# Splitting the bit-by-bit top-k search of a sparse-attention layer into three groups instead of two

## The chip, the cores and the metric

The kernel runs on one core of one Trainium2 chip. The metric is the device time of one execution in microseconds (us). The kernel before was timed in 3 runs: 1661.65, 1662.74 and 1662.96 us, a median of 1662.74 us. A separate execution was recorded by the hardware profiler. A core has five engines that each work through a queue of their own in order: PE (matrix products), DVE (vector work), ACT (activation functions, casts and copies), POOL (more vector work) and SP (which issues transfers).

## The reference, cut to what matters

The layer has two attention branches, a gate for each and a feed-forward part. Branch A attends sparsely: an indexer scores every key for every query, and only the best `topk` keys take part. There are 1024 prompt positions (topk 256) and 32 sample positions that also see a cache of 512 keys (topk 136).

```python
def dsa_block(q, q_i, w_i, qpos, k, v, k_i, topk):
    s_idx = jnp.einsum('bqhd,bld->bqhl', q_i, k_i).astype(jnp.float32)
    score = jnp.einsum('bqhl,bqh->bql', jax.nn.relu(s_idx), w_i.astype(jnp.float32))
    admissible = (kpos // CHUNK)[None, :] <= (qpos // CHUNK)[:, None]
    score = jnp.where(admissible[None], score, -jnp.inf)
    _, idx = lax.top_k(score, topk)
    ...
    p = jax.nn.softmax(logits, axis=-1)
    return jnp.einsum('bqhk,bqkhd->bqhd', p.astype(v.dtype), vg)
```

Everything else (the projections, the second branch, the gates, the feed-forward part) is dense matrix work around this.

## The kernel before, in words

The 1056 positions are cut into 9 tiles: tiles 0 to 7 hold 128 prompt positions each, and tile 8 holds the 32 sample positions. Query tile t of the prompt sees 128(t+1) keys, and tile 8 sees 544. Tiles 0 and 1 have at most 256 keys and need no search. For tiles 2 to 8 the kernel makes the scores (`index_scores`, line 955): PE writes products into three PSUM banks called `s`, ACT applies relu in place, and DVE adds the weighted result into a `score` tile. Tiles 2, 3, 4 and 8 come first there, and 5, 6 and 7 later.

Then it finds for each query the k-th largest score by setting the 31 bits of a float from the top down (`top_k_begin`, line 984). For each bit DVE makes a candidate threshold (`cand`, an xor on the threshold `thr`), the scores below it are counted for each tile, DVE compares the counts with what is wanted (`hit`), and `thr` takes the candidate where the comparison holds (`copy_predicated`). `thr`, `hit` and the wanted counts lie in a PSUM tile called `small`. A count is a pass over a tile's scores: on DVE a compare with an accumulated sum, followed by a read of the accumulator; on ACT a sign function with an accumulated sum. Tiles 5, 6 and 7, the longest, are counted on ACT, and 2, 3, 4 and 8 on DVE.

The tiles are put in groups, and one candidate, one comparison and one conditional copy serve all tiles of a group, side by side in its columns. The table `TOPK` (line 53) names each group, its tiles, those of them that ACT counts, and its place in `small`. Before there are two groups: "a" with tiles 2, 3, 4 (DVE) and 7 (ACT), and "b" with 5 and 6 (ACT) and 8 (DVE). So each group's comparison waits for counts of both engines. After the search `top_k` (line 1053) turns each threshold into a mask, tile by tile, in the order of the groups: a few passes on ACT and, on DVE, a scan and a comparison into the tile `pre`, with one more pair of passes into `pen` for tiles that ACT counted.

The order of all instructions is made when the program is built. Every operation is recorded with a rank (FAST for emptying PSUM, PREP for loads, MAIN, FILL for matrix products that fill PE's time, SLOW for the search), and a list scheduler (`Plan.run`, line 371) lets each engine take the ready operation of the best rank, by a table of costs. On the chip each engine then runs its list strictly in that order. While the search runs, PE makes the dense projections: of branch B and the first gates (`project_b`, `gate`) and then of branch A (`project_a`). Their results lie in two PSUM banks `pj` (and the three `s`), and DVE empties them in rows whose outputs are called `zb`, `vt`, `gz` and `ta`; these are called evictions below and are counted from the start of the program. Branch B's attention starts after the masks are done, its k, q, v and weight tiles use the memory that the search frees.

Of the kernel before, what the change touches and what calls it, by code (L numbers as in the profile page):

```python
# [49 lines left out]
FWORDS = 3200  # L50
PACE = 16
PA_BANKS = ('s', 'pj', 's', 's', 'pj')
TOPK = (("a", [2, 3, 4, 7], (7,), 0), ("b", [5, 6, 8], (5, 6), 16))
QUARTER = T // 4
QUADS = ((QUARTER, 0), (QUARTER, 2 * QUARTER))
B11, B21, T1, T2, T3, T4, B22 = range(7)
# [404 lines left out]
class Layer:  # L461
# [522 lines left out]
    def top_k_begin(self):  # L984
# [59 lines left out]

        self.groups = [Group(*x) for x in TOPK]
        self.size = size
# [1004 lines left out]
```

## Time and profile before

| | us |
|---|---|
| median of 3 runs | 1662.74 |
| the profiled execution, its own time | 1660.59 |
| the span of its instructions | 1658.8 |
| PE busy in the span | 1648.2 (99%) |
| DVE busy in the span | 1296.7 (78%) |
| ACT busy in the span | 988.7 (60%) |
| first search count on DVE that reads a candidate (start) | 176.0 |
| last search count on DVE (start) | 336.0 |

The span runs from the first to the last instruction of the program; the execution's own time has 1.79 us around it. A row of a timeline gives a start and a duration in us, the engine, the operation, what it writes and reads by the program's names (`junk<-score,cand` is a count, `small<-cnta,small` the comparison of group a, `small<-small,cand` the conditional copy), the shapes, and in brackets how long the engine sat idle before it and what released it. Nearly all rows stand under line 441, since one helper issues every operation. Rows of matrix products overlap each other, so the pace of PE is read from one start to the next.

### The profile page before, as it was taken

How to read it: one execution, taken by the hardware profiler on the slowest of the kernel's cores; microseconds unless marked ns; L12 is line 12 of the kernel's file. 1: busy time of each engine (PE TensorE's matmuls, PEld its weight loads, DVE VectorE, ACT ScalarE, POOL GpSimd, SP SyncE). 2: the span in 40 equal slices, each digit the busy share in tenths (PEclk: the TensorE clock that was granted, in tenths of full speed). 3: DMA queues.
4: the chain of work that ended last, by engine and by line, in shares of the span. 5: the costliest groups of instructions: out<-in, count | busy, mean ns of one | idle time of the engine just before them, and what ended most of it. 6: DMA issues, size and time to landing. Idle time of an engine off the chain costs nothing.

```text
span 1658.8 us, 34178 instructions
## 1 busy us (share of the span) xinstructions
PE 1648.2 (99%) x12226; PEld 1580.1 (95%) x12226; DVE 1296.7 (78%) x2683; ACT 988.7 (60%) x1999; POOL 594.2 (36%) x523
## 2 busy tenths in 40 slices
PE   9999999999999999999999999999999999999999
PEld 9988999999989999989999999999999999999999
DVE  6777899987479889777877559888887777577686
ACT  7556889765376777897765446455555654343431
POOL 4522333344246576245556238333332200000000
PEclk9999999999999999999999999999999999999999
DMA  8243464355474645788764533444444696676674
GB/s 287 62 136 99 144 187 155 108 172 149 138 217 113 175 125 157 195 255 250 240 197 155 182 113 120 158 143 146 147 143 149 218 337 225 189 253 198 207 220 138
DMA packets 178649, 290.25 MB, mean 175 GB/s; under 512 B 28688, under 2 KB 55536, under 8 KB 178448
## 3 DMA queue, kind: packets, MB, share of 16 engines
q1 hardware_dynamic: 178192, 287.91, 55.7%
q8 instruction: 96, 1.57, 0.4%
q14 instruction: 73, 0.60, 0.1%
q10 hardware_dynamic: 288, 0.17, 0.0%
HBM read 195.09 MB, written 94.90 MB: 175 GB/s over the span
## 4 chain that ended last, share of the span: by engine, by line
PE 89%; DVE 6%; DMA 2%; issue 1%; ACT 1%; POOL 1%; SPq 0%; DVEq 0%; ACTq 0%; POOLq 0%
PE pj L441 34%; PE c L441 15%; PE b L441 12%; PE s L441 10%; PE a L441 9%; PE t L441 5%; PE o L441 5%; DVE junk L441 2%; DMA wst<-w_g 1%; DMA wst<-w_bb 0%; DVE small L441 0%; DVE ta L441 0%; DVE y L441 0%; SPq L441 0%; DMA xl<-do 0%
## 5 line engine op out<-in xcount | busy, mean ns | idle before, releaser
L441 PE MATMUL pj<-xl,wh 128*128 128x272 f32 (+2 forms) x1056 | 298.8, 313 | 0.0
L441 PE MATMUL pj<-xh,wh 128*128 128x272 f32 (+1 forms) x696 | 227.5, 327 | 0.0
L441 PE MATMUL pj<-xh,wl 128*128 128x272 f32 (+1 forms) x696 | 226.7, 326 | 0.0
L441 POOL TENSOR_TENSOR wl<-wst,wh 128x512 fp32r<-128x512 f32 x104 | 149.6, 1443 | 151.2 <-ACT wh L441 138.5
L441 PEld LDWEIGHTS pj<-xl,wh 128*128 128x128 f32 x1056 | 188.1, 188 | 9.7
L441 ACT CAST wh<-wst 128x512 fp32r<-128x512 f32 x192 | 117.5, 620 | 128.5 <-PE c L441 29.1
L441 PEld LDWEIGHTS pj<-xh,wl 128*128 128x128 f32 x696 | 131.0, 188 | 9.1
L441 PEld LDWEIGHTS pj<-xh,wh 128*128 128x128 f32 x696 | 131.0, 188 | 9.0
L441 PE MATMUL c<-mh,wh 128*128 128x264 f32 (+1 forms) x688 | 132.3, 284 | 0.7 <-DVE ft L441 0.7
L441 POOL TENSOR_TENSOR p<-p,rem 128x127 f32<-128x127 f32 (+8 forms) x66 | 99.8, 1523 | 77.2 <-DVE rem L441 37.0
L441 ACT CAST wh<-us 128x512 fp32r<-128x512 f32 x81 | 50.3, 621 | 121.8 <-PE a L441 32.0
L441 PE MATMUL b<-oa,wh 128*128 128x264 f32 x624 | 116.5, 284 | 0.0
L441 DVE TENSOR_TENSOR tt<-t,tt 128x512 fp32r<-128x512 f32 (+2 forms) x168 | 100.2, 618 | 14.8 <-ACT tt L441 13.8
L441 DVE TENSOR_TENSOR_SCAN rem<-rem,first 128x128 f32<-128x128 f32 (+8 forms) x66 | 109.1, 1667 | 3.2 <-ACT rem L441 3.1
L441 PEld LDWEIGHTS c<-mh,wh 128*128 128x128 f32 x688 | 108.1, 188 | 1.0 <-DVE ft L441 0.9
L441 PE MATMUL c<-mh,wl 128*128 128x264 f32 (+1 forms) x368 | 104.6, 284 | 0.0
L441 ACT ACTIVATE junk<-score,cand 128x1024 bf16<-128x1024 f32 (+2 forms) x93 | 96.9, 1042 | 11.0 <-DVE cand L441 9.4
L441 ACT CAST tt<-t 128x512 fp32r<-128x512 f32 (+2 forms) x168 | 86.3, 541 | 26.3 <-PE t L441 19.3
L441 PE MATMUL o<-tt,v 128*128 128x256 f32 (+1 forms) x640 | 97.5, 278 | 0.6 <-ACT tt L441 0.4
L441 PE MATMUL s<-k,q 128*128 128x512 f32 (+4 forms) x384 | 95.9, 350 | 1.1 <-DMA q<-dq 1.0
L441 PEld LDWEIGHTS b<-oa,wh 128*128 128x128 f32 x624 | 96.8, 188 | 0.0
L441 DVE TENSOR_TENSOR wl<-wst,wh 128x512 fp32r<-128x512 f32 x88 | 69.4, 792 | 34.2 <-ACT wh L441 33.7
(439 smaller groups left out, 5358.9 us busy)
## 6 DMA issues: line engine op xcount, KB each, us to landing
us<-w_down SPq DMA_DIRECT2D x80, 256.0 KB, 3.4
q<-dq SPq DMA_DIRECT2D x64, 256.0 KB, 4.4
du<-us SPq DMA_DIRECT2D x56, 264.0 KB, 3.2
du<-y SPq DMA_DIRECT2D x56, 264.0 KB, 2.1
y<-w_up SPq DMA_DIRECT2D x45, 256.0 KB, 3.0
k<-dk SPq DMA_DIRECT2D x40, 256.0 KB, 4.4
v<-dv SPq DMA_DIRECT2D x40, 256.0 KB, 4.3
xl<-du SPq DMA_DIRECT2D x32, 264.0 KB, 4.2
```

The source lines that it names most:

```text
L441: fn(*args, **kw)
```

## The change

One line of the table of groups changes. Tile 8 moves to group "a", which is now counted by DVE alone; tile 7 moves to "b" beside tile 5, and tile 6 gets a group "c" of its own, so that "b" and "c" are counted by ACT alone. Which engine counts which tile stays as it was.

```diff
-TOPK = (("a", [2, 3, 4, 7], (7,), 0), ("b", [5, 6, 8], (5, 6), 16))
+TOPK = (("a", [2, 3, 4, 8], (), 0), ("b", [7, 5], (7, 5), 16), ("c", [6], (6,), 32))
```

A third group means a third candidate, comparison and conditional copy for every bit. And the scheduler orders the program anew: DVE, ACT, POOL, SP and PE all get another order between the late score products and the end of `project_a`. PE's list is the same before its matrix product 849 (at 130.4 us of the profile before) and from product 3022 (at 442.4 us) to the end.

On DVE, in the scoring stage, the list from eviction 31 to eviction 32 was this before: only scores between them (`score_1269` and `score_1271` are those of tiles 5 and 7).

```order
L441 TENSOR_TENSOR zb<-pj,rb 128x512
L441 SCALAR_TENSOR_TENSOR score_1269<-s,wi,score_1269 128x256
L441 SCALAR_TENSOR_TENSOR score_1271<-s,wi,score_1271 128x512
L441 SCALAR_TENSOR_TENSOR score_1269<-s,wi,score_1269 128x256
L441 SCALAR_TENSOR_TENSOR score_1271<-s,wi,score_1271 128x512
L441 SCALAR_TENSOR_TENSOR score_1269<-s,wi,score_1269 128x256
L441 TENSOR_TENSOR zb<-pj,rb 128x272
```

The same place now, from the same eviction to the next:

```order
L441 TENSOR_TENSOR zb<-pj,rb 128x512
L441 SCALAR_TENSOR_TENSOR score_1271<-s,wi,score_1271 128x512
L441 SCALAR_TENSOR_TENSOR score_1269<-s,wi,score_1269 128x256
L441 SCALAR_TENSOR_TENSOR score_1271<-s,wi,score_1271 128x512
L441 TENSOR_SCALAR junk,cnta_1464<-score_1267,cand 128x512
L441 TENSOR_SCALAR junk,cnta_1464<-score_1268,cand 128x640
L441 TENSOR_TENSOR zb<-pj,rb 128x272
```

Two of the five scores have made room for counts of tiles 3 and 4: group a's search stands among the scores of tiles 5 and 7, since it no longer needs them. Between evictions 28 and 37 DVE has 5 counts and 9 operations on candidates, comparisons and copies before, and 25 and 18 after.

On DVE, in the middle of the search, one bit of group a was this before:

```order
L441 TENSOR_SCALAR junk,cnta_1464<-score_1266,cand 128x384
L441 TENSOR_TENSOR zb<-pj,rb 128x272
L441 TENSOR_SCALAR junk,cnta_1464<-score_1267,cand 128x512
L441 TENSOR_SCALAR junk,cnta_1464<-score_1268,cand 128x640
L441 TENSOR_TENSOR small<-cntb_1469,small 128x3
L441 COPY_PREDICATED small<-small,cand 128x3
L441 TENSOR_SCALAR cand<-small 128x3
L441 TENSOR_SCALAR junk,cntb_1468<-score_1272,cand 32x544
```

And now:

```order
L441 TENSOR_SCALAR junk,cnta_1464<-score_1266,cand 128x384
L441 TENSOR_TENSOR small<-cntc_1472,small 128x1
L441 TENSOR_SCALAR junk,cnta_1464<-score_1267,cand 128x512
L441 COPY_PREDICATED small<-small,cand 128x1
L441 TENSOR_SCALAR junk,cnta_1464<-score_1268,cand 128x640
L441 TENSOR_SCALAR cand<-small 128x1
L441 TENSOR_SCALAR junk,cnta_1464<-score_1272,cand 32x544
L441 TENSOR_TENSOR zb<-pj,rb 128x512
```

The small operations of group c stand singly between group a's counts. Between evictions 37 and 61 DVE has 86 counts and 126 small operations before, and 94 and 183 after.

On DVE, in `project_a`, around an eviction of a `pj` bank late in the search, the list was this before:

```order
L441 TENSOR_SCALAR junk,cnta_1464<-score_1268,cand 128x640
L441 COPY_PREDICATED small<-small,cand 128x3
L441 TENSOR_SCALAR cand<-small 128x3
L441 TENSOR_SCALAR junk,cntb_1468<-score_1272,cand 32x544
L441 TENSOR_TENSOR ta<-pj,tabc 128x256
L441 TENSOR_REDUCE ss<-sq 128x4
L441 TENSOR_TENSOR tb<-pj,tabs 128x256
L441 TENSOR_TENSOR small<-cnta_1464,small 128x4
```

In the first part of `project_a` it now reads:

```order
L441 TENSOR_TENSOR small<-cntb_1468,small 128x2
L441 COPY_PREDICATED small<-small,cand 128x2
L441 TENSOR_REDUCE ss<-sq 128x4
L441 TENSOR_SCALAR cand<-small 128x2
L441 TENSOR_TENSOR ta<-pj,tabc 128x256
L441 TENSOR_TENSOR tb<-pj,tabs 128x256
L441 TENSOR_TENSOR small<-cntc_1472,small 128x1
```

Group a is through by then: between evictions 61 and 78 DVE has 33 counts and 52 small operations before, and 5 and 69 after. The two remaining groups end later than before: twelve of their small operations stand between evictions 78 and 84 (before: three), and the last pass of the masks on DVE stands behind eviction 102 instead of 98.

## The prediction

> **What bounds the kernel now.** I read the page's table of engines first, then the waits of PE while the search runs, then the busy time of the engines by stretches.
>
> ```profile
> span 1658.8 us, 34178 instructions
> PE 1648.2 (99%) x12226; PEld 1580.1 (95%) x12226; DVE 1296.7 (78%) x2683; ACT 988.7 (60%) x1999; POOL 594.2 (36%) x523
> ```
>
> PE is busy for all but 10.6 us of the span, and the change takes no matrix product away and adds none. So time can only come from PE's waits, and be lost in new ones. PE's list is unlike the old one only between 130.4 and 442.4 us; these are all its waits there (who waited for whom: total, times, longest):
>
> ```profile
> PE t L441 <- POOL qk L441: 1.1, 1, 1.1
> PE pj L441 <- DVE small L441: 0.7, 1, 0.7
> ```
>
> Next the busy time in stretches, cut at the starts of the evictions 28, 37, 61 and 78 (129.3, 181.3, 282.8 and 337.8 us), two later ones (379.8 and 411.1) and the point from which PE's list is the old one. The columns are the length, then the busy time of PE, PEld, DVE, ACT and POOL.
>
> ```profile
> 129.30:181.30 52.00, 52.00 (x310) 46.67 (x309) 37.15 (x76) 34.00 (x68) 13.80 (x15) 1.00 0.40 114
> 181.30:282.80 101.50, 101.50 (x655) 93.01 (x654) 94.63 (x339) 91.19 (x180) 32.94 (x32) 1.00 0.54 166
> 282.80:337.80 55.00, 53.11 (x420) 51.19 (x418) 51.56 (x187) 42.40 (x88) 24.92 (x26) 1.00 0.43 128
> 337.80:379.80 42.00, 41.86 (x330) 40.56 (x331) 35.90 (x84) 25.10 (x55) 20.32 (x19) 1.00 0.53 161
> 379.80:411.10 31.30, 31.20 (x241) 29.79 (x241) 26.57 (x60) 17.88 (x38) 12.97 (x12) 1.00 0.49 138
> 411.10:442.40 31.30, 31.30 (x235) 29.77 (x234) 20.31 (x52) 12.15 (x30) 13.11 (x14) 1.00 0.45 138
> ```
>
> Two things are to be seen. PE's idle time here is 0 + 0 + 1.89 + 0.14 + 0.10 + 0 = 2.13 us: that is the most that a better order can give, 0.13% of the time. And DVE, which empties PE's banks, is the engine with the least room: 14.85 us idle in the first stretch, 6.87 in the second, 3.44 in the third. The granted clock (the column 1.00) is full throughout.
>
> **The change part by part.** It moves DVE's search forward and adds small operations to it. From the order: between evictions 28 and 37 there are 20 more counts and 9 more small operations; between 37 and 61, 8 and 57 more; between 61 and 78, 28 counts fewer and 17 small operations more. In all 95 small operations are added (285 against 190). The prices come from the rows of the counts, grouped by shape, with their accumulator reads, and from the busy time of the operations on `small` and `cand` in the stretches (the rows of the tile `small`: length, DVE busy, times).
>
> ```profile
> L441 DVE TENSOR_SCALAR_CACHE_REDUCE junk<-score,cand 128x640 bf16<-128x640 f32 x31 | 27.0, 872 | 0.4
> L441 DVE TENSOR_SCALAR_CACHE_REDUCE junk<-score,cand 32x544 bf16<-32x544 f32 x31 | 23.7, 765 | 0.8
> L441 DVE TENSOR_SCALAR_CACHE_REDUCE junk<-score,cand 128x512 bf16<-128x512 f32 x31 | 23.0, 743 | 0.8
> L441 DVE TENSOR_SCALAR_CACHE_REDUCE junk<-score,cand 128x384 bf16<-128x384 f32 x31 | 18.9, 611 | 0.9
> L441 DVE DVE_READ_ACCUMULATOR junk<-score,cand 128x1 f32 x93 | 7.6, 82 | 0.0
> L441 DVE DVE_READ_ACCUMULATOR junk<-score,cand 32x1 f32 x31 | 2.2, 71 | 0.0
> ```
> ```profile
> 181.30:282.80 101.50, 20.27 (x126) 1.00 0.54 166
> ```
>
> A count costs (27.0 + 23.7 + 23.0 + 18.9 + 7.6 + 2.2) / 124 = 0.83 us, a small operation that stands by itself 20.27 / 126 = 0.16 us. But not all stand by themselves. Here are two counts that follow each other directly, and two with one small operation between them (DVE's timeline):
>
> ```profile
> 176.62 0.75 DVE L441 TENSOR_SCALAR_CACHE_REDUCE junk<-score,cand 128x512 bf16<-128x512 f32 x1
> 177.29 0.08 DVE L441 DVE_READ_ACCUMULATOR junk<-score,cand 128x1 f32 x1
> 177.41 0.88 DVE L441 TENSOR_SCALAR_CACHE_REDUCE junk<-score,cand 128x640 bf16<-128x640 f32 x1
> ```
> ```profile
> 181.90 0.74 DVE L441 TENSOR_SCALAR_CACHE_REDUCE junk<-score,cand 128x512 bf16<-128x512 f32 x1
> 182.56 0.08 DVE L441 DVE_READ_ACCUMULATOR junk<-score,cand 128x1 f32 x1
> 182.56 0.16 DVE L441 TENSOR_TENSOR small<-cntb,small 128x3 int32<-128x3 f32 x1
> 182.68 0.88 DVE L441 TENSOR_SCALAR_CACHE_REDUCE junk<-score,cand 128x640 bf16<-128x640 f32 x1
> ```
>
> From start to start it is 0.79 us without and 0.78 us with the small operation: it runs beside the accumulator's read and costs nothing. In the new order 34 small operations stand singly between two counts in the second stretch, against 5 before, and most of the others in runs of both groups' operations, which do not wait for each other.
>
> Against the change speaks the Trainium skill, "VectorE: DVE Perf Modes", section "Rules for kernel authors": it advises to make chained DVE operations fewer, because each one's drain is paid in any case. The Trainium skill's "Perfetto Trace Analysis", section "Optimizing Scalar/DVE Operations", puts the overhead of one on PSUM at about 125 ns, by which the 95 would be an estimated 11.9 us of DVE's time; by the two rows at 182.56 a single one costs none.
>
> *First stretch, 129.3 to 181.3 us.* Added: 20 x 0.83 + 9 x 0.16 = 18.0 us, against 14.85 us idle. DVE is over-full by 3.2 us. Where this lies decides: an eviction that is late costs PE nothing as long as PE still has the other `pj` bank to fill. Its 24 matrix products of 272 columns start 0.125 us apart,
>
> ```profile
> 448.00 0.29 PE L441 MATMUL pj<-xh,wl 128*128 128x272 f32 x1
> 448.13 0.29 PE L441 MATMUL pj<-xh,wh 128*128 128x272 f32 x1
> ```
>
> so one bank is a cover of 24 x 0.125 = 3.0 us. The score products have three smaller banks and a shorter cover, and they share this stretch. So I bound the loss between 0 (all covered) and 3.2 us (nothing covered), and take 1.0: nearer the cover, which is as long as the overrun. Part of the idle time has been waiting for ACT's relu and may not be usable:
>
> ```profile
> DVE score L441 <- ACT s L441: 9.5, 18, 1.1
> ```
>
> but an engine that is behind no longer meets such waits, so I do not add it.
>
> *Second stretch, 181.3 to 282.8 us.* Added: 8 x 0.83 = 6.6 us of counts and 57 small operations, from 0 (all hidden) to 57 x 0.16 = 9.1 us (none); together 6.6 to 15.7 us against 6.87 idle: between 0.3 us to spare and 8.8 us over. I take the hidden end, because of the rows at 182.56 and because a small operation between two counts also takes away the gap of 0.12 us between them. The loss of PE then is small: 0.3 us for an eviction here and there behind a full queue.
>
> *Third stretch, 282.8 to 337.8 us.* Removed: 28 x 0.83 = 23.2 us; added 17 x 0.16 = 2.7 us. DVE goes from 3.44 us idle to some 24. Both of PE's waits lie here, or at its end:
>
> ```profile
> 309.86 0.33 PE L441 MATMUL t<-ident,qk 128*128 128x128 f32 x1 [1.09 <-POOL qk L441]
> 337.92 0.36 PE L441 MATMUL pj<-wh,xh 128*128 128x256 f32 x1 [0.72 <-DVE small L441]
> ```
>
> The first is a transpose that waits for POOL's sum `qk`, and POOL for DVE's `tb`, which stands behind counts; the second is a `pj` bank whose readers `ta` and `tb` stand behind a count. Without counts there both should go: a gain of 1.09 + 0.72 = 1.8 us, bounded by 0 and the 2.13 us of the stretches.
>
> *After the search, 337.8 to 442.4 us.* The passes for the masks come in another sequence, and later. By the order, 379.8 to 411.1 us has the penalty passes of 1024 and of 768 columns on DVE in addition, and three scans as before. Their rows:
>
> ```profile
> L441 DVE TENSOR_SCALAR pen<-score,tfa 128x1024 f32<-128x1024 f32 x1 | 0.7, 743 | 0.0
> L441 DVE CUSTOM_DVE_ANT_0 pen<-pen,score 128x1024 f32<-128x1024 f32 x1 | 1.2, 1216 | 0.0
> L441 DVE TENSOR_SCALAR pen<-score,tfb 128x768 f32<-128x768 f32 x1 | 0.6, 609 | 0.0
> L441 DVE CUSTOM_DVE_ANT_0 pen<-pen,score 128x768 f32<-128x768 f32 x1 | 2.0, 2036 | 0.0
> ```
>
> That is 4.6 us more against 4.73 us idle: DVE is just full there, and I put the loss of PE between 0 and 1 us and take 0.2. DVE's last mask pass moves by four evictions and stays ahead of 442.4 us, from where PE's list is the old one. The counts on ACT are the same 96, and ACT has 10.3 us idle in the second stretch and 12.6 in the third. SP and POOL change places of a few rows only, and no transfer is added.
>
> *Sum.* -1.8 + 1.0 + 0.3 + 0.2 = -0.3 us. The profiled execution took 1660.59 us for its span of 1658.8; it would take 1660.3. The runs' median, 1662.74, lies 2.15 us above it, so the forecast is 1662.74 - 0.3 = 1662.4 us: no change, PE bound as before. A measurement of this kernel can tell about 0.2%, 3.3 us, from no change. The likeliest case's own range is 1660.0 (all 2.13 us gained, and half a microsecond from run to run) to 1665.0 (losses of 3.2 and 0.9, less the gain).
>
> **The rivals.**
>
> *DVE over-full through the first half (slower).* If the small operations are not hidden, DVE owes 3.2 + 8.8 = 12.0 us by eviction 61, and an eviction behind it makes PE wait once the debt passes one bank's cover, 3.0 us. PE loses 12.0 - 3.0 = 9.0, gains the 1.8: 1662.74 + 7.2 = 1669.9 us. For it: DVE is 93% busy in the second stretch already, and the added groups are ready there in plenty. Against it: the pair of rows at 182.56. It decides from 3.0 us of debt on. Chance 0.19. By the Trainium skill's advice on fewer operations ("VectorE: DVE Perf Modes", "Rules for kernel authors") this is the case to expect; the two rows at 182.56 do not agree with it.
>
> *DVE stuck behind ACT (a little slower).* In the third stretch DVE's list has comparisons of groups b and c, which wait for counts on ACT, ahead of evictions of `project_a`. Before, no wait of DVE for a count shows; these are all its waits of 181 to 338 us:
>
> ```profile
> DVE tb L441 <- ACT sq L441: 2.0, 4, 0.5
> DVE gz L441 <- PE pj L441: 0.8, 2, 0.5
> DVE zb L441 <- PE pj L441: 0.7, 1, 0.7
> DVE vt L441 <- PE pj L441: 0.2, 1, 0.2
> ```
>
> Now ACT's counts there are the only thing the search waits for. One such wait is at most about one count long, some 1.2 us, below a bank's cover; a stall as long as the old one at 309.86 could stay. Then the gain of 1.8 falls away, and 1.0 + 0.3 + 0.2 remain: 1664.2 us. Chance 0.12.
>
> *The gain is all and no loss (faster).* Every wait goes, and the fewer handovers give as much again: 2 x 2.13 = 4.3 us, 1658.4 us. Only the first half of this is in any row. Chance 0.04.
>
> That the change does nothing to the order is excluded by the order itself; that it matters behind 442.4 us is not, but PE's list is the same there.
>
> **How the numbers follow.** The forecast case has 0.65. It lies within 0.2% nearly always: I give 0.61 to the same, 0.02 to faster and 0.02 to slower. The stuck DVE gives 0.10 to the same and 0.02 to slower, the over-full DVE 0.19 to slower, the last 0.04 to faster. In sum faster 0.06, same 0.71, slower 0.23. For 8 in 10 the range runs from 1659.5 (below it most of the faster rival) to 1668.5, which takes in the lower part of the over-full case and leaves its upper part, about 0.12, out.
>
> **What would show it.** In the profile after, PE should have no wait near 309 and 338 us; DVE should be about full from 129 to 283 us, and clearly idler from 283 to 338; the start of the 61st eviction should lie at 283 to 285 us. If it lies 5 us or more later, the over-full case is right, and PE's waits between 130 and 283 us will name DVE. If PE's time before 283 us is unchanged and waits for POOL or DVE stand in `project_a` with DVE idle before comparisons, it is the stuck case. A difference that arises behind 442 us would make the whole argument wrong.

## The result: 8.6 us slower, and the profile after

The changed kernel takes 1671.45 us (median of 6 runs, 1670.5 to 1675.3) against 1662.85 us for the kernel before on the same chip (6 runs, 1661.65 to 1664.63). The ratio is 1.0055 with a 95% interval of 1.0044 to 1.0065. The forecast was 1662.4 us and no change; the range ended at 1668.5. What happened is the first rival, a DVE that is over-full while the search runs.

The profiled execution after took 1671.93 us, with a span of 1670.2 us. First the page's table of engines:

```profile
span 1670.2 us, 34284 instructions
PE 1652.3 (99%) x12226; PEld 1582.2 (95%) x12226; DVE 1307.7 (78%) x2780; ACT 988.6 (59%) x1999; POOL 594.3 (36%) x523
```

Then all waits of PE between 130 and 450 us, the part in which its list is new:

```profile
PE t L441 <- DVE vt L441: 6.4, 5, 2.3
PE pj L441 <- DVE gz L441: 0.4, 1, 0.4
```

The two old waits (POOL's `qk`, DVE's `small`) are gone, as forecast. In their place stand five waits in which PE's transposes of `vt` wait for the eviction that writes `vt`, and a short one on `gz`.

The stretches, cut at the starts of the same evictions (28, 37, 61, 78), the last row reaching to the product from which PE's list is the old one (length, then busy time of PE, PEld, DVE, ACT and POOL, then the granted clock and two columns of transfers that are not used here):

```profile
129.78:181.37 51.59, 51.59 (x308) 46.21 (x307) 49.72 (x124) 31.26 (x63) 13.82 (x15) 1.00 0.40 115
181.37:292.56 111.19, 105.57 (x663) 95.52 (x661) 105.78 (x412) 83.32 (x162) 32.21 (x31) 0.98 0.50 152
292.56:345.83 53.27, 51.99 (x414) 50.47 (x415) 36.82 (x147) 46.90 (x100) 25.59 (x27) 1.00 0.45 132
345.83:386.42 40.59, 40.59 (x321) 39.36 (x320) 31.88 (x82) 26.70 (x62) 17.02 (x19) 1.00 0.50 149
386.42:422.70 36.28, 36.28 (x284) 35.03 (x283) 31.86 (x66) 20.12 (x41) 17.57 (x13) 1.00 0.52 150
422.70:450.00 27.30, 27.27 (x200) 25.53 (x199) 20.23 (x51) 13.33 (x28) 13.01 (x14) 1.00 0.47 140
```

All that is lost up to 450.0 us is lost in the second stretch: 111.19 us in place of 101.50, 9.7 us more. The first takes 51.59 (52.00 before), the third 53.27 (55.00), and all behind it up to 450.0 us 104.2 (104.6). The 61st eviction starts at 292.56 us, where the forecast had 283 to 285.

Why the second stretch grew is in DVE's waits inside it (181 to 293 us). This is the only one:

```profile
DVE zb L441 <- PE pj L441: 0.6, 1, 0.6
```

DVE never waits but for those 0.6 us, which end at the stretch's start. It is the bound of the stretch, and PE follows it. What DVE has more to do shows in the rows of the tile `small` (length, DVE's busy time, times), which were 20.27 us in 126 operations:

```profile
181.37:292.56 111.19, 29.89 (x183) 0.98 0.50 152
```

DVE's busy time grows by 11.15 us (94.63 to 105.78): 5.9 for the counts with their reads (the tile `junk`, 65.25 to 71.15 us), 9.6 for small operations, less 4.4 in which rows lie over each other (its other work is the same to within 0.4 us). DVE's idle time shrinks by 1.46 us (6.87 to 5.41). The difference of the two, 9.69 us, is what the stretch grew by, as it must be: a stretch is DVE's busy time plus its idle time.

### The profile page after: what moved, and what is told of

It is laid out like the page before. It is cut to its first block, busy times and chain, and to the rows that moved or that the text cites. A ratio compares the mean times of both kernels' runs of the same rounds, so it can differ in the third digit from the quotient of the medians.

```text
span 1670.2 us, 34284 instructions
## 1 busy us (share of the span) xinstructions
PE 1652.3 (99%) x12226; PEld 1582.2 (95%) x12226; DVE 1307.7 (78%) x2780; ACT 988.6 (59%) x1999; POOL 594.3 (36%) x523
## 4 chain that ended last, share of the span: by engine, by line
PE 86%; DVE 8%; DMA 3%; issue 2%; ACT 1%; POOL 0%; SPq 0%; DVEq 0%; ACTq 0%; POOLq 0%
PE pj L441 31%; PE c L441 14%; PE b L441 11%; PE s L441 10%; PE a L441 9%; PE t L441 5%; PE o L441 5%; DVE junk L441 3%; DVE small L441 1%; DMA x<-xT 1%; DMA q<-dq 1%; DVE qi L441 1%; DVE ml L441 0%; DVE wl L441 0%; DVE cand L441 0%
## 5 line engine op out<-in xcount | busy, mean ns | idle before, releaser
L441 PE MATMUL c<-mh,wl 128*128 128x264 f32 (+1 forms) x368 | 104.6, 284 | 0.0
```

Of the source, the lines that this page charges most:

```text
L441: fn(*args, **kw)
```

## The experiments

My theory was the first rival: DVE has more to do in the second stretch than it has time, through counts that run ahead and through small operations that are not hidden. The rivals: the early start of group a alone costs, with the counts that it puts ahead of evictions (A); PE suffers only because its transposes stand too close behind their eviction (B); the one-column conditional copy costs (C); and, as the deeper cause, the planner prices the search's operations too low and so packs DVE too full (D). Each of the ten kernels was timed in five rounds beside the kernel before, whose medians were 1661.76 to 1661.95 us.

### Two groups, the first on DVE alone

```diff
-TOPK = (("a", [2, 3, 4, 8], (), 0), ("b", [7, 5], (7, 5), 16), ("c", [6], (6,), 32))
+TOPK = (("a", [2, 3, 4, 8], (), 0), ("b", [7, 5, 6], (7, 5, 6), 16))
```

> Two groups again, but the first one as in the changed kernel: a with tiles 2, 3, 4, 8 on DVE alone, b with 7, 5, 6 on ACT alone. Group a still starts early and runs ahead (127 counts by the 61st eviction by the order, 95 before the change, 123 after it); the third set of small operations is gone (146 by the 61st eviction; 144 before, 214 after). DVE over-full by counts and small operations together: 32 counts x 0.83 + 2 x 0.16 = 26.9 us more than before up to the 61st eviction against 21.7 us idle, 5.2 us over, less a cover of 3.0: some 2 us of PE's waits, two old waits of 1.8 us gone: 1662.5 to 1665, the 61st eviction at 283 to 287 us. If the early start itself (counts ahead of evictions) is what costs: 1669 to 1672 as in the changed kernel.

1665.97 us, ratio 1.0023 (1.0014 to 1.0032); the 61st eviction starts at 287.92 us. Group a starts as early as in the changed kernel and has more counts ahead of that eviction, yet more than half of the loss is gone. A is not the cause, though counts ahead cost something. The time is 1 us above what the theory gave. The 61st eviction is 5.1 us late, as much as the whole 5.2 that I had DVE over-full, with no cover taken off; but this is chance. The 28th eviction is already 1.25 us late (130.53 us), ahead of everything that changed in PE's list, and the 5.2 counted idle time as room that was none, as told below.

### Three groups of both engines

```diff
-TOPK = (("a", [2, 3, 4, 8], (), 0), ("b", [7, 5], (7, 5), 16), ("c", [6], (6,), 32))
+TOPK = (("a", [2, 3, 7], (7,), 0), ("b", [4, 5], (5,), 16), ("c", [6, 8], (6,), 32))
```

> Three groups, each with tiles of both engines (a 2, 3 and 7; b 4 and 5; c 8 and 6), so that no group starts before the late scores: 285 small operations in the bits as in the changed kernel, but 96 counts by the 61st eviction as before the change (95) and 217 small operations (214 after, 144 before). DVE over-full: between the 37th and the 61st eviction 2 counts and 69 small operations more, 1.7 + 11.0 = 12.7 us against 6.9 idle, 5.9 over, less 3.0 of cover: 2.9 us lost, 1664.5 to 1667, PE's waits of 130 to 300 us on vt. If the early start costs and small operations are hidden beside the accumulator's read: 1662 to 1663.5.

1674.65 us, ratio 1.0074 (1.006 to 1.0089): no early start, no counts ahead, and slower than the changed kernel. The 61st eviction starts at 289.00 us, 6.2 us late, where 5.9 were worked out without a cover; that is near in part by luck, since the 5.9 took all idle time as room and priced every small operation in full, two errors that about cancel here. The time is 8 us above the expected range. The rest is lost in the third stretch, 58.83 us in place of 55.00, where this kernel still searches, and in the next one, 44.65 us in place of 42.00, in which the granted clock fell to half for 3.4 us. These are PE's longest waits of 120 to 460 us:

```profile
PE t L441 <- DVE vt L441: 5.3, 8, 1.7
PE pj L441 <- DVE tb L441: 2.2, 1, 2.2
PE s L441 <- DVE tb L441: 1.8, 1, 1.8
```

The rows on `tb` are the banks of `project_a`, which a full DVE empties late.

### The changed kernel with group a held back

```diff
+        a = self.groups[0]
+        nc.vector.tensor_scalar(a.zero, score[7][:, 1020:1024], 0.0, None, op0=ALU.mult)
         for g in self.groups:
             g.step(g.zero, ALU.is_gt, g.allb)
```

> The changed kernel, but group a's zero is made from four columns of tile 7's score (times 0.0), so that its search cannot start before the late scores: the stretch up to the 37th eviction has 9 counts and 25 small operations (before 9 and 18, after 29 and 31), that from the 37th to the 61st has 94 counts and 180 small operations, as in the changed kernel (94 and 183; before 86 and 126). DVE over-full by the unhidden small operations of this one stretch: 8 x 0.83 + 54 x 0.16 = 15.3 us against 6.9 idle, 8.4 over, less 3.0 of cover: 5 us lost, 1666 to 1669. If the early start costs: 1662 to 1664. If small operations are hidden: 1662 to 1663.5 as well.

1672.24 us, ratio 1.0062 (1.0048 to 1.0076), as slow as the changed kernel and 3 us above the expected range; the 61st eviction starts at 293.27 us. So the search's early part in the first stretch has no share in the loss, and the second stretch makes all of it: from the 37th eviction (182.25 us) it is 111.02 us long, 9.5 more than before, where the expectation had 8.4 less 3.0.

### The transposes later in PE's list

```diff
...
+        n.late = 3000 if op == "transpose" and ins[0].tensor.name.startswith("vt") else 0
...
-        return d.end + (STORE if n.store else SLACK) + (70 if n.eng in (PE, POOL) else 45)
+        return d.end + n.late + (STORE if n.store else SLACK) + (70 if n.eng in (PE, POOL) else 45)
```

> The changed kernel, but the scheduler takes the transposes of vt to be ready 3.0 us later, so that PE's list has some 15 to 25 more products ahead of them; DVE's list is nearly the same (123 counts and 214 small operations by the 61st eviction, as in the changed kernel). DVE over-full: the debt of DVE stays, and PE meets it at the pj banks or at vt a little later: 1667 to 1671, losing at most one more cover of 3 to 4 us. If PE only suffers because the transposes stand too close behind their eviction, and one pj bank would have covered the rest: the waits of 6.4 us on vt go and nothing takes their place, 1663 to 1665.

1677.09 us, ratio 1.0088 (1.0072 to 1.0103), 6 us above the expected range. The 61st eviction starts at 292.34 us, 0.2 us from the changed kernel, and PE's longest waits of 130 to 450 us have only changed their name:

```profile
PE pj L442 <- DVE vt L442: 3.9, 3, 1.7
PE pj L442 <- DVE zb L442: 1.4, 1, 1.4
PE pj L442 <- DVE gz L442: 1.2, 2, 0.6
```

The wait on `vt` was where DVE's lateness showed, not its cause: B falls. Why this kernel is some 5.5 us slower still than the changed one is only partly told. In the profiled executions PE is 2.6 us later than there at product 3022, and no more than that at its last product. But the profiled execution, 1674.54 us, is the fastest of this kernel's six, and what the others lose besides no trace shows.

### A third set of small operations alone, in the kernel before

```diff
...
             for g in self.groups:
                 g.bit(b)
+            cand = nc.tile(tp, [128, 1], I32, "cand", tag="candx", bufs=2)
+            nc.vector.tensor_scalar(cand, thr, 1 << b, None, op0=ALU.bitwise_xor)
+            nc.vector.tensor_tensor(hit, self.groups[0].cnts[0][:, 0:1], want, op=ALU.is_le)
+            nc.vector.copy_predicated(thr, hit, cand)
```

(`thr`, `hit` and `want` are columns of `small` that nothing else uses.)

> The kernel before, with its two groups and its split, plus a third candidate, comparison and one-column conditional copy for every bit, that counts nothing: the comparison reads group a's first count. By the order the counts stay where they were (94 by the 61st eviction, 95 before) and 213 small operations stand ahead of it (144 before, 214 after). DVE over-full, by what the runs so far show: a first small operation behind a count is free, each further one costs some 0.2 us, and of the 6.9 us that DVE idles in the second stretch 5.0 are gaps of about 35 ns between instructions, so 1.8 are room: 63 more small operations at 0.07 (the price in the changed kernel's trace, 3.9 us for 57) are 4.4 us, at 0.16 10 us; less 1.8: the 61st eviction 2.6 to 8 us later, 285.5 to 291, the time 1665 to 1671. If the counts that run ahead of the evictions are the whole cause: no change, 1661.5 to 1663.

1676.21 us, ratio 1.0087 (1.0073 to 1.0101). The 61st eviction starts at 290.32 us, within the expected 285.5 to 291. These are the second stretch, with all engines, and the rows of `small` in it:

```profile
182.70:290.32 107.62, 103.61 (x656) 93.08 (x654) 101.43 (x402) 89.95 (x178) 32.08 (x31) 1.00 0.51 157
182.70:290.32 107.62, 30.42 (x189) 1.00 0.51 157
```

Groups and split are the old ones here, and the stretch has 85 counts where there were 86. So small operations alone do it: 63 more of them make the stretch 6.1 us longer, and the assumption that they are hidden is shown to be wrong. The time is 5 us above the expected range. The loss goes on in the third stretch, 58.44 us in place of 55.00, as with the three mixed groups. In the profiled execution, at 1680.11 us the slowest of the six, another 9.6 us come behind product 3022, with 10.2 us at half the granted clock and longer waits for a transfer and for `ft`; that is far from the search.

### Group c two columns wide

```diff
-                n = len(tiles)
+                n = max(2, len(tiles))
...
+                nc.vector.memset(g.want, 0.0)
```

> The changed kernel with group c two columns wide (the second one idle), so that its conditional copy has the form of the other groups' (164 to 170 ns) in place of the one-column form (222 ns). If that form is what costs: 31 x 0.055 = 1.7 us less, 1669.7. DVE over-full by number and place of the operations: the same within 1 us, 1670.5 to 1672.

1672.39 us, ratio 1.0063 (1.0051 to 1.0076): no gain, C is not the cause. All one-column copies are gone, those of two columns take 165 ns, and the second stretch is 109.81 us long, 1.4 less than in the changed kernel. So the form is at most a small part of what overfills DVE, and the time does not show it.

### The planner's prices, for the whole program

```diff
+            if "accum_out" in kw or n <= 4:
+                d += 100
             return d - 70, d
```

Once in the changed kernel, and once in the kernel before.

> The changed kernel, planned with 100 ns more for every accumulating DVE operation and every one of at most four columns (planned 0.68 us for a 512-column count and 0.08 for a small operation, measured 0.79 and some 0.2 from start to start). By the order 92 counts and 180 small operations stand ahead of the 61st eviction (123 and 214 without, 95 and 144 before the change), and the search lasts to the 89th. If the planner overfills DVE because it prices these operations too low: 3 counts fewer and 36 small operations more than before, -2.5 + 36 x 0.07 = 0.0 us up to the 61st eviction, which starts at 283 to 285; the waits on vt go; 1662 to 1665. If a third set of small operations costs its DVE time wherever it stands: 1668 to 1672.

> The kernel before with the same 100 ns more in the plan: 83 counts and 126 small operations ahead of the 61st eviction (95 and 144 without), the search ends at the 88th eviction and the masks at the 114th (98 without). DVE has some 10 + 2 us more room up to the 61st, where PE already lost nothing; the two waits near 309 and 338 us may stay, since the search now stands beside them longer: 1661 to 1664, no change. If the plan's prices are what makes every order bad: below 1660.

1670.49 us, ratio 1.0047 (1.0035 to 1.0059), and 1666.81 us, ratio 1.0027 (1.0018 to 1.0036). Both times miss their expectations, and the first lies where it would if a third set cost its time wherever it stands. And yet the 61st eviction starts at 283.54 us, within the expected 283 to 285, and at 283.07 us where the kernel before has the new prices. The edit also prices small operations behind the search and so makes another list for PE there. Against the profile of before, the two lie 3.9 and 0.9 us behind at product 5000 (727 us) and 10.0 and 6.7 us behind at product 6000 (870 us): some 6 us of each loss arise there, far from the search. These two runs tell of the second stretch alone.

### The planner's prices, for the search alone

```diff
+            if self.level[-1] == SLOW and ("accum_out" in kw or n <= 4):
+                d += 50
             return d - 70, d
```

> The changed kernel, planned with 50 ns more for the search's accumulating DVE operations and its operations of at most four columns, and for these alone, so that PE's list is the old one from product 3028 on. By the order 106 counts and 204 small operations stand ahead of the 61st eviction (123 and 214 without, 95 and 144 before the change), of them 79 and 176 behind the 37th (before 86 and 126). DVE over-full as the cause: -7 x 0.83 + 50 x 0.07 = -2.3 us against before in that stretch, so the 61st eviction starts at 282.5 to 285 us and PE's waits on vt there go to below 2 us; the search's rest, 22 counts and some 80 small operations, then stands beside project_a's first rows, where DVE had 3.4 us idle: 0 to 3 us lost there. 1662 to 1666. If a third set of small operations costs its time wherever it stands: 1670 to 1672 as in the changed kernel.

> The kernel before with the same 50 ns in the plan: 88 counts and 138 small operations ahead of the 61st eviction (95 and 144 without), PE's list the old one from product 3028 on. DVE has 7 x 0.83 + 6 x 0.07 = 6.2 us more room where PE lost nothing already: no gain there; the two old waits near 309 and 338 us may go or stay: 1660.5 to 1663. If the plan's prices cost the kernel before something as well: below 1660.

The changed kernel with these prices takes 1664.88 us (12 runs), within the expected 1662 to 1666, ratio 1.0014 (1.0005 to 1.0023). By the ratios three quarters of the loss are gone with the same three groups; by the medians 3.1 of 8.6 us are left. Its stretch up to the 61st eviction, and PE's waits of 130 to 450 us:

```profile
181.02:281.83 100.81, 100.81 (x650) 92.38 (x649) 93.99 (x375) 84.58 (x165) 33.31 (x32) 1.00 0.54 167
```
```profile
PE s L443 <- DVE small L443: 0.4, 1, 0.4
PE t L443 <- POOL qk L443: 0.4, 1, 0.4
PE pj L443 <- DVE tb L443: 0.2, 1, 0.2
PE t L443 <- DVE vt L443: 0.2, 1, 0.2
```

PE has no idle time in the stretch. DVE is 93.99 us busy, 0.6 less than in the kernel before, with 50 more small operations and 7 fewer counts; the counts stand later, beside `project_a`. D is shown by this edit of the prices alone: the third group costs little where the plan leaves room for it, and much where the plan thinks DVE has room that it has not. By the planner's formula a count of 512 columns occupies DVE for 160 + 512 + 80 - 70 = 682 ns and a small operation for 81 to 94; the trace has 790 and some 200 from start to start.

The kernel before with these prices takes 1660.91 us (12 runs), ratio 0.9993 (0.9984 to 1.0001): the fastest of all, but not told apart from no change. That the old plan left room at the old prices I put down to group a's comparisons, which waited for ACT's counts of tile 7 and so kept the search from filling DVE; no run takes this apart.

## Why the prediction was wrong, point by point

**The gain, -1.8: right.** Both waits went, and the third stretch is 1.73 us shorter. That the size fits so well is partly chance, since the stretch now begins inside a wait of PE's and holds 414 products in place of 420.

**The first stretch, +1.0: too high, nothing was lost.** DVE's busy time grew by 12.6 us (37.15 to 49.72), not by 18.0: the added rows come to 17.9 us, but rows now lie over each other by 5.4 us more. The 14.85 us of idle time held that, and it was real: 9.5 us of it were waits for ACT's relu, as the prediction's row shows, and another 4.9 were waits for PE's banks.

**The second stretch, +0.3: the step that failed, three times over.**

First, "6.87 us idle" was taken as room. It was not. The rows to tell it stood in the prediction: DVE's waits there, on banks that PE had not filled, are `gz` 0.8, `zb` 0.7 and `vt` 0.2, together 1.7 us. The other 5.2 us are gaps between one instruction's end and the next one's start, and the changed kernel, in which DVE waits for 0.6 us, still shows 5.41. With 1.7 of room the 8 counts alone, 6.6 us, overfill the stretch; as measured, with the overlap of a count and its read, they are 5.9.

Second, "I take the hidden end" for the small operations. The pair of rows at 182.56 was read rightly but stood for the wrong case. A single operation between two counts is free in the changed kernel too (DVE's timeline):

```profile
242.71 0.61 DVE L441 TENSOR_SCALAR_CACHE_REDUCE junk<-score,cand 128x384 bf16<-128x384 f32 x1
243.25 0.08 DVE L441 DVE_READ_ACCUMULATOR junk<-score,cand 128x1 f32 x1
243.25 0.16 DVE L441 TENSOR_TENSOR small<-cntc,small 128x1 int32<-128x1 f32 x1
243.37 0.75 DVE L441 TENSOR_SCALAR_CACHE_REDUCE junk<-score,cand 128x512 bf16<-128x512 f32 x1
```

But where the operations of several groups come together at the end of a bit, only the first is free:

```profile
236.11 0.76 DVE L441 TENSOR_SCALAR_CACHE_REDUCE junk<-score,cand 32x544 bf16<-32x544 f32 x1
236.80 0.07 DVE L441 DVE_READ_ACCUMULATOR junk<-score,cand 32x1 f32 x1
236.80 0.15 DVE L441 TENSOR_TENSOR small<-cntc,small 128x1 int32<-128x1 f32 x1
236.98 0.16 DVE L441 TENSOR_SCALAR cand<-small 128x2 int32<-128x2 int32 x1
237.18 0.23 DVE L441 COPY_PREDICATED_SCALAR small<-small,cand 128x1 int32 x1
237.44 0.17 DVE L441 TENSOR_TENSOR small<-cnta,small 128x4 int32<-128x4 f32 x1
237.64 0.16 DVE L441 TENSOR_SCALAR cand<-small 128x1 int32<-128x1 int32 x1
237.83 0.17 DVE L441 COPY_PREDICATED small<-small,cand 128x4 int32<-128x4 int32 x1
238.03 0.16 DVE L441 TENSOR_SCALAR cand<-small 128x4 int32<-128x4 int32 x1
238.23 0.61 DVE L441 TENSOR_SCALAR_CACHE_REDUCE junk<-score,cand 128x384 bf16<-128x384 f32 x1
```

From the end of the count at 236.87 to the next at 238.23 the seven take 1.36 us, 0.2 us for each but the first, whether or not one depends on the one before. In the stretch 46 of the 183 stand singly; the other 137 make runs of two to eight. Of the 9.6 us that the 57 added ones are busy, 9.6 - 4.4 = 5.2 came on DVE's path, near the middle of the 0 to 9.1 that the prediction had. Counted by the rule it would be somewhat more: 108 of them stand right behind another one, where there were 74, and 34 x 0.2 = 6.8. By the Trainium skill's "Perfetto Trace Analysis", section "Optimizing Scalar/DVE Operations", 125 ns each, the 57 would be an estimated 7.1 us; the trace lies below it, since singles are free. The Trainium skill's advice against this change ("VectorE: DVE Perf Modes", "Rules for kernel authors") agrees with the runs: every kernel here with a third set of small operations is slower than the kernel before.

Third, "an eviction that is late costs PE nothing" within one bank's cover of 3.0 us. With the two sizes above DVE was over-full by 6.6 + 5.2 - 1.7 = 10.1 us, and the stretch grew by 9.7. The 5.2 comes from this very trace, so that is bookkeeping and no test; the run with group a held back, by the same prices, has 6.6 + 54 x 5.2 / 57 - 1.7 = 9.8, and its stretch grew by 9.5. Nothing of it was covered for good: at product 3022 PE is 7.6 us late, which is the 9.7 and 0.5 from ahead of the 28th eviction, less the 2.5 that the other stretches gained. This is how DVE and PE stand at one of the waits:

```profile
245.08 0.77 DVE L441 TENSOR_SCALAR_CACHE_REDUCE junk<-score,cand 32x544 bf16<-32x544 f32 x1
245.78 0.07 DVE L441 DVE_READ_ACCUMULATOR junk<-score,cand 32x1 f32 x1
245.78 0.67 DVE L441 TENSOR_TENSOR vt<-pj,rb 128x512 f32<-128x512 f32 x1
246.39 0.14 DVE L441 TENSOR_TENSOR small<-cntb,small 128x2 int32<-128x2 f32 x1
```
```profile
246.51 0.66 PE L441 MATMUL t<-ident,vt 128*128 128x128 f32 x4 [1.99 <-DVE vt L441]
```

The eviction waits behind counts that the plan put ahead of it, and PE's transposes read its output at once; a second `pj` bank is no help to them. With the transposes moved the banks ran out instead. A cover can be spent once; it does not pay for a queue that is too long throughout the stretch.

**The masks, +0.2: nothing was lost.** From the 78th eviction to product 3022 the kernel takes 104.2 us, before 104.6.

**The rivals.** The over-full DVE was forecast at 1669.9 us; its figure is near for the wrong sum, 12.0 of debt less 3.0 of cover, where the runs show 9.7 and no cover. Its mark, the 61st eviction 5 us late or more with PE's waits on DVE, came true. The rival of a DVE stuck behind ACT's counts played no part in PE's waits, though DVE itself waited for such counts five times behind the second stretch, 2.3 us in all.

**Behind 442 us** the prediction allowed no difference. PE is 7.6 us late at product 3022 and 11.4 at the end, in these two executions. But the two kernels with 50 ns in the plan, which have the same list for PE there, also lose 2.3 and 2.2 us behind that product against the same profile of before, which lies 2.2 us below its median. What remains, about 1.5 us, is no more than the halved clock told of below can explain. The loss behind that product differs much between profiles whatever the search does (0.1 us with group a held back, 4.0 with two groups), so that its size here is not shown to belong to the change.

## What to carry to other kernels

Idle time of an engine is room only as far as the view of its waits accounts for it: an engine that is 93% busy and waits for 1.7 us in 100 is full. An operation that is free in one place, beside a read that follows a long operation, has its price again as soon as two of them stand together, so count runs and not instructions. And where a list scheduler fills an engine, a change that gives it more ready work needs prices that are right, since the operations that were priced too low are put ahead of the ones that others wait for.

## What the runs showed of the hardware

A wait can slow TensorE after it. Behind PE's wait of 1.99 us, which ended at 246.51, the granted clock fell to half (the first column behind POOL's) for 3.41 us, and 272-column products started 0.23 us apart in place of 0.13. The first two rows are the stretch up to the fall and the one at half; the third is a stretch with a longer wait and no fall behind it:

```profile
243.71:247.12 3.41, 1.42 (x12) 1.21 (x11) 3.31 (x13) 2.61 (x7) 0.76 (x1) 1.00 0.37 106
247.12:250.53 3.41, 3.41 (x17) 3.41 (x16) 3.34 (x14) 2.70 (x6) 0.00 (x0) 0.50 0.17 39
291.49:294.91 3.42, 1.61 (x13) 1.61 (x14) 3.18 (x13) 3.21 (x9) 1.54 (x2) 1.00 0.00 0
```
```profile
247.13 0.43 PE L441 MATMUL pj<-xl,wh 128*128 128x272 f32 x1
247.36 0.43 PE L441 MATMUL pj<-xh,wl 128*128 128x272 f32 x1
...
250.53 0.29 PE L441 MATMUL pj<-xl,wh 128*128 128x272 f32 x1
250.66 0.28 PE L441 MATMUL pj<-xh,wl 128*128 128x272 f32 x1
```

The same followed the second of these waits, far from the search, where it costs the changed kernel some 1.7 us (half of 3.41) of the difference behind 442 us. The first, the longer one, was not followed by it:

```profile
293.30 0.66 PE L441 MATMUL t<-ident,vt 128*128 128x128 f32 x4 [2.34 <-DVE vt L441]
915.70 0.52 PE L441 MATMUL c<-xl,wh 128*128 128x272 f32 x2 [1.95 <-DVE ft L441]
```

The traces show what decides. In each of the twelve profiles the clock's records change only at the ends of equal windows of 3.413 us: the falls at 247.12 and 916.13 lie 669.01 us apart, which is 196 of them. With the program's end left aside, the clock fell behind the seven windows in which PE was idle, by its rows, for 1.83 to 2.17 us, and behind none of those with 1.81 us or less. The wait that ended at 293.30 was cut by a window's end at 291.49, so that 0.53 us of it lay in one window and 1.81 in the next. A fall thus needs a window that is idle for a little more than half, and whether a wait of 2 us meets that is a matter of where it lies. The Trainium skill's "TensorE: Matmul & The Clock Gate", Part 1, has the clock drop after an idle window of about 3.4 us that runs freely. The window and its free run agree with these traces; but here a window that was busy for 1.42 us was enough, and the measurement decides. Inside the second stretch the fall costs little of its own, since DVE sets the time there: the kernel with the transposes later has no fall in that stretch, and it is 110.84 us long, 0.35 less.

The conditional copy of one column takes another form, and a slower one, than those of two or four (in the changed kernel; behind the first bar stand the total in us and the mean in ns, behind the second the idle time before them):

```profile
L441 DVE COPY_PREDICATED_SCALAR small<-small,cand 128x1 int32 x31 | 6.9, 222 | 0.5
L441 DVE COPY_PREDICATED small<-small,cand 128x4 int32<-128x4 int32 x31 | 5.3, 170 | 1.0
L441 DVE COPY_PREDICATED small<-small,cand 128x2 int32<-128x2 int32 x31 | 5.1, 164 | 0.6
```
